# The output projection's first 512 columns computed with tokens as rows and held in PSUM

## The chip, the cores and the metric

The kernel runs on one core of a Trainium2 chip. Its time is the device time of one execution in microseconds (us), the median of three runs. Engines are named as the profile names them: PE is TensorE (PEld its weight loads), DVE is VectorE, ACT is ScalarE, POOL is GpSimd, SP is SyncE, whose queue issues most of the transfers. SBUF is the on-chip memory of 128 partitions; PSUM is the memory of eight banks that PE writes, a bank being 128 partitions by 512 fp32 values.

## What is computed

The reference is one step of a decoder layer: an input projection, a chunked mLSTM branch, a sliding-window attention branch, a gated merge, an output projection, a residual and a layer norm. There are 512 prompt tokens and 8 x 4 = 32 sample tokens, and the model is 2048 wide. The end of it, which the change touches, reads:

```python
y = (sigmoid(g_m) * einsum('btc,cd->btd', br_m, w_proj_m)
     + sigmoid(g_a) * einsum('btc,cd->btd', br_a, w_proj_a))
out = einsum('btc,cd->btd', y, w_out)
return layernorm(DN_ALPHA * x + out, ln_w, ln_b)
```

All inputs are fp32.

## The kernel before

All 544 tokens (T = 512 + 32) go through the projections together. Activations are held with channels on the partitions, `[128 channels, tokens]`, 16 such tiles along k for 2048 channels. An fp32 product is made of three fast products in a rounded fp32 form: an operand is split into a high part, cast by ACT (L208 for weights), and a low part, the difference made by DVE (L209); then high x high, high x low and low x high are added in PSUM.

A plain column tile (`gemm`, L232) takes 128 columns of a weight. It loads them in two halves of 8 k (`load_half`, L197, 128 x 8 x 128 values in pieces of 128 columns, on SP's queue; pool `wr`, three buffers), splits each half (`split`, L202, two buffers each of high and low parts), and issues 8 k x 3 x 2 products a half (`products`, L213): the weights are stationary, and the 544 tokens move as two runs of 272 columns (L218), each into a PSUM bank of its own.

Most column tiles come in pairs of 256 columns (`paired`, L732): each pair is computed by seven half-size products instead of eight, numbered 0 to 6, out of sums of weight blocks and sums of activations. `prepare` (L670) makes the weight sums (DVE L679, and POOL transfers that add, L677) and splits them, up to three products ahead; `half_product` (L691) issues 16 products with the high weight part (L699), then 8 with the low one (L701), all of 272 columns; `gather` (L703) combines the banks on ACT, POOL and DVE. A pair uses three banks.

PSUM is two pools of four banks: `sm` for small results and `bank` for the projections. Background work is written as generators that are started by `spawn` and advanced by `tick` (L134), which the loops over products call. The instructions of each engine are put in order by a scheduler that runs a time model over the program; what is written under `tc.high_priority` (weight preparation, offset `AHEAD`) is drawn ahead. Each engine then executes strictly in that order, and so does SP's queue.

Around the change the program runs like this. The last two merged tiles of y (k = 14, 15) are plain tiles of w_proj_m; meanwhile `back` (L1891) reads the first 14 tiles of y from DRAM and splits them into `yh`, `yl` (hi and lo). Then the output projection begins with four plain tiles of w_out (columns 0 to 511). They only need y itself, and during them `operand_sums` (L1692) reads y again and makes the sums that the pairs need. Each of the four results is copied out of PSUM by ACT (L1919) and stored to DRAM (`d_o`, L1920). Then come four pairs (columns 512 to 1535). In their background `plain_back` (L2059) loads each of the four results again, and `add_residual` (L1950) turns it by PE transposes (L1956 for the four blocks of 128 prompt tokens, L1963 for the 32 samples) and adds it to ALPHA times the rows of x: `z0` (prompt rows, columns 0 to 511) and 32 partitions of `zs` (samples), loaded by `load_rows` (L1940, L1941). The first layer norm statistics follow (L1969). The end of the kernel (columns 1536 to 2047, the norm, the stores) comes after the pairs; three of its column tiles are computed for the prompt with tokens as stationary rows and weights moving, 384 columns at a time (L2049).

Of the kernel before, what the change touches and what calls it, by code (L numbers as in the profile page):

```python
# [21 lines left out]
SEQ = 512  # L22
# [52 lines left out]
def _build(tc, nc, i, o, es):  # L75
# [38 lines left out]
    def ev(n=T):  # L114
        return evp.tile([128, n], F32, tag="ev", name=nm("ev"))
# [27 lines left out]
    def drain():  # L143
        while live:
            tick()
# [86 lines left out]
    def gemm(wv, c0, xh, xl, cols=EVEN, raws=(None, None), every=8, prio=0, before=None, parts=(1, 1),  # L232
             ps=None, behind=None, pins=(None, None), splits=None):
        ps = ps or mm()
        for half in range(2):
            if before:
                before(half)
            if splits:
                products(ps, half, *splits[half], xh, xl, cols, every[half] if isinstance(every, tuple) else every)
                continue  # L240
            raw = raws[half] or load_half(wv, c0, half)
            if prio:
                with tc.high_priority(offset=prio):
# [19 lines left out]
    def whole(tiles):  # L263
        return lambda k, c, w: tiles[k // 4][:, k % 4, c:c + w]
# [1402 lines left out]
    def c5t():  # L1667
        return c5.tile([128, T], F32, tag="c5", name=nm("c5"))
# [218 lines left out]
    tx = pool(esE, "ty", 6)  # L1887
    yh_, yl_ = act_tiles(act, "yh"), act_tiles(act, "yl")
    yh, yl = whole(yh_), whole(yl_)

    def back():  # L1891
        for k in range(14):
            t_ = tx.tile([128, T], F32, tag="ty", name=nm("ty"))
            nc.sync.dma_start(t_[:], d_y[k])
            hilo(t_[:], yh_[k // 4][:, k % 4], yl_[k // 4][:, k % 4])
            if k % 2:
                yield

    spawn(back())
    for ct in range(14, 16):  # L1900
        merge = merged(ct, plain=True)
        sg = merge([p_[:, :HT] for p_ in gemm(wm, ct * 128, bmh, bml, every=4, prio=AHEAD)])
        nc.sync.dma_start(d_y[ct], sg[:])
        hilo(sg[:], yh_[ct // 4][:, ct % 4], yl_[ct // 4][:, ct % 4])
    drain()
    esE.close()

# [4 lines left out]
    tx = pool(esT, "txd", 3)  # L1912
    Y = {}
    spawn(operand_sums(d_y, Y, act3, 3))
    for ct in range(4):
        ps = gemm(wo, ct * 128, yh, yl, every=4, prio=AHEAD)
        ot = ev()
        for p_, o_ in halves(ps, ot):
            A.copy(o_, p_)  # L1919
        nc.sync.dma_start(d_o[ct], ot[:])  # L1920
    drain()
    esT.close()

# [132 lines left out]
                nc.sync.dma_start(d_o[c], o[:])  # L2056
        return end

    def plain_back():  # L2059

        for ct in range(4):
            t_ = c5t()
            with tc.issue_after(state["load"].ins):
                nc.sync.dma_start(t_[:], d_o[ct])
            for _ in range(5):
                yield
            add_residual(ct, t_, 0, 5)
        yield
        stats(0, 4, 0)

# [15 lines left out]
        load_ln()  # L2086

    load_rows(0)
    spawn(plain_back())
# [150 lines left out]
```

## Time and profile before

| | us |
|---|---|
| median of three runs | 2443.71 |
| lowest and highest run | 2440.34, 2447.24 |
| the profiled execution's own time | 2442.73 |
| its span in the profile | 2440.9 |
| four plain tiles of w_out, from the first product | 2236.84 to 2284.6 |
| four pairs of w_out | 2284.8 to 2371.35 |

A line of the profile names the source line, the engine, the operation, and output<-input tiles without buffer numbers, then partitions x elements. In a timeline the first two numbers are start and duration in us. Matmuls are pipelined: a product of 272 columns is shown with 0.29 us, but one starts every 0.125 us, so the distance between starts is what one costs. A fp32 product of full precision shows as two records.

### The profile page before, as it was taken

How to read it: one execution, taken by the hardware profiler on the slowest of the kernel's cores; microseconds unless marked ns; L12 is line 12 of the kernel's file. 1: busy time of each engine (PE TensorE's matmuls, PEld its weight loads, DVE VectorE, ACT ScalarE, POOL GpSimd, SP SyncE). 2: the span in 40 equal slices, each digit the busy share in tenths (PEclk: the TensorE clock that was granted, in tenths of full speed). 3: DMA queues.
4: the chain of work that ended last, by engine and by line, in shares of the span. 5: the costliest groups of instructions: out<-in, count | busy, mean ns of one | idle time of the engine just before them, and what ended most of it. 6: DMA issues, size and time to landing. Idle time of an engine off the chain costs nothing.

```text
span 2440.9 us, 49025 instructions
## 1 busy us (share of the span) xinstructions
PE 2425.6 (99%) x19394; PEld 2372.5 (97%) x19394; DVE 1910.2 (78%) x2879; ACT 1252.0 (51%) x2074; POOL 533.8 (22%) x509
## 2 busy tenths in 40 slices
PE   8999999999999999999999999999999999999998
PEld 8999999999999999999999999999999999999997
DVE  7768888888888888887877888878865676877666
ACT  6456676666666665443433444444654444434432
POOL 3114333333333431211111121120000120111111
PEclk9999999999999999999999999999999999999999
DMA  6876766667767655577687677587864588898776
GB/s 179 197 178 155 164 157 156 153 155 178 167 169 177 164 141 159 153 221 231 192 255 232 174 231 225 174 245 217 264 204 148 186 236 265 233 235 270 199 218 205
DMA packets 569597, 479.88 MB, mean 197 GB/s; under 512 B 48664, under 2 KB 464136, under 8 KB 569112
## 3 DMA queue, kind: packets, MB, share of 16 engines
q1 hardware_dynamic: 550776, 411.22, 56.9%
q0 software_dynamic: 18112, 64.76, 13.5%
q8 instruction: 152, 2.49, 0.4%
q10 hardware_dynamic: 480, 0.79, 0.1%
q14 instruction: 77, 0.63, 0.1%
HBM read 326.35 MB, written 100.77 MB: 175 GB/s over the span
## 4 chain that ended last, share of the span: by engine, by line
PE 97%; DMA 2%; DVE 1%; ACT 0%; issue 0%; SPq 0%; DVEq 0%; POOLq 0%; ACTq 0%
PE bank L699 49%; PE bank L701 24%; PE bank L218 10%; PE sm L1529 2%; PE bank L1335 1%; PE sm L1568 1%; PE sm L814 1%; PE sm L1584 1%; PE sm L865 1%; PE sm L218 1%; PE sm L2049 1%; DMA raw<-raw 1%; PE sm L840 1%; PE sm L1340 1%; DMA raw<-in_w_out 1%; DMA raw<-in_w_proj_a 0%
## 5 line engine op out<-in xcount | busy, mean ns | idle before, releaser
L208 ACT CAST wh<-raw 128x1024 fp32r<-128x1024 f32 x641 | 671.8, 1048 | 822.4 <-PE bank L699 697.1
L209 DVE TENSOR_TENSOR wl<-raw,wh 128x1024 fp32r<-128x1024 f32 x641 | 801.2, 1250 | 198.8 <-ACT wh L208 185.6
L699 PE MATMUL bank<-xk,wh 128*128 128x272 f32 x2336 | 323.4, 289 | 0.0
L679 DVE TENSOR_TENSOR raw<-raw,raw 128x1024 f32<-128x1024 f32 x244 | 310.9, 1275 | 9.7 <-DMA raw<-in_w_proj_a 2.3
L699 PEld LDWEIGHTS bank<-xk,wh 128*128 128x128 f32 x2336 | 303.4, 188 | 1.9 <-issue 1.4
L718 POOL TENSOR_TENSOR ev<-p,ev 128x272 f32<-128x272 f32 x85 | 117.7, 1384 | 453.2 <-ACT ev L717 429.7
L699 PE MATMUL bank<-n2h,wh 128*128 128x272 f32 x656 | 170.0, 291 | 0.0
L699 PE MATMUL bank<-n3h,wh 128*128 128x272 f32 x656 | 169.5, 291 | 0.3 <-ACT wh L208 0.2
L701 PE MATMUL bank<-xk,wl 128*128 128x272 f32 x1168 | 169.8, 287 | 0.0
L699 PE MATMUL bank<-s1h,wh 128*128 128x272 f32 x656 | 169.6, 291 | 0.0
L699 PE MATMUL bank<-n2l,wh 128*128 128x272 f32 x656 | 168.0, 287 | 0.0
L699 PE MATMUL bank<-n3l,wh 128*128 128x272 f32 x656 | 167.6, 288 | 0.0
L699 PE MATMUL bank<-s4h,wh 128*128 128x272 f32 x656 | 167.5, 289 | 0.0
L699 PE MATMUL bank<-s1l,wh 128*128 128x272 f32 x656 | 167.4, 287 | 0.0
L699 PE MATMUL bank<-s4l,wh 128*128 128x272 f32 x656 | 167.0, 287 | 0.0
L701 PEld LDWEIGHTS bank<-xk,wl 128*128 128x128 f32 x1168 | 155.5, 188 | 0.1
L677 POOL DMA_DIRECT2D raw<-raw x96 | 83.2, 866 | 320.3 <-DVE ev L726 209.9
L699 PE MATMUL bank<-a11h,wh 128*128 128x272 f32 x584 | 150.4, 289 | 0.0
L699 PE MATMUL bank<-a11l,wh 128*128 128x272 f32 x584 | 149.4, 288 | 0.0
L699 PEld LDWEIGHTS bank<-n3h,wh 128*128 128x128 f32 x656 | 123.4, 188 | 2.2 <-issue 1.2
L699 PEld LDWEIGHTS bank<-s1h,wh 128*128 128x128 f32 x656 | 123.2, 188 | 1.6 <-issue 1.0
L699 PEld LDWEIGHTS bank<-n2h,wh 128*128 128x128 f32 x656 | 123.4, 188 | 1.2 <-issue 1.2
(552 smaller groups left out, 5800.2 us busy)
## 6 DMA issues: line engine op xcount, KB each, us to landing
raw<-in_w_in SPq DMA_DIRECT2D x296, 512.0 KB
raw<-raw POOLq DMA_DIRECT2D x96, 512.0 KB, 5.0
C<-in_state_mlstm_C SPq DMA_DIRECT2D x32, 1024.0 KB
out<-C SPq DMA_DIRECT2D x64, 512.0 KB
raw<-in_w_proj_a SPq DMA_DIRECT2D x32, 512.0 KB
raw<-in_w_proj_m SPq DMA_DIRECT2D x32, 512.0 KB
raw<-in_w_out SPq DMA_DIRECT2D x32, 512.0 KB
d_v<-ev SPq DMA_DIRECT2D x16, 272.0 KB
```

Source lines behind the costliest of these rows:

```text
L208: state["cast"] = A.copy(wh[:, k:k + n], raw[:, k:k + n])
L209: state["split"] = V.tensor_tensor(out=wl[:, k:k + n], in0=raw[:, k:k + n], in1=r32(wh[:, k:k + n]), op=ALU.subtract)
L218: PE.matmul(ps[f][:, :w], a[:, kk], b(k, c, w), start=(k == 0 and n == 0), stop=(k == 15 and n == 2))
L677: state["summed"] = G.dma_start(out=w[out][:], in_=w[b][:], accum_op=ALU.add)
L679: V.tensor_tensor(out=w[out][:], in0=w[a][:], in1=w[b][:], op=ALU.add)
L699: PE.matmul(ps, wh[:, k], x(p, k), start=(first and k == 0 and p == 0), stop=False, skip_group_check=True)
L701: state["end"] = PE.matmul(ps, wl[:, k], x(0, k), start=False, stop=(k == 7), skip_group_check=True)
L718: G.tensor_tensor(out=c22, in0=p1, in1=c11, op=ALU.subtract)
L814: PE.matmul(pp[:, c0 + w0:c0 + 256], qs[a][:, j * 128:j * 128 + 128], kx[:, k0:k0 + 256 - w0], start=(n == 0), stop=(n == 1))
L840: PE.transpose(pt[:, b * 128:b * 128 + 128], s_[:, b, 128:256], ident)
L865: PE.matmul(po[:, b * 128:b * 128 + n], VA[:, b], p_[:, 2 * b:2 * b + n // 128], start=(b == 0 and m == 0), stop=(b == 3 and m == 1), skip ...
L1529: state["cells"] = PE.matmul(pp[:, 0:258], a[:, b * 128:b * 128 + 128], b_[:, b, f], start=(b == 0 and n == 0), stop=(b == 3 and n == 2))
```

## The change

The four plain tiles of w_out are replaced by one wide stage with tokens as rows:

- The weight is loaded in eight blocks of two k by all 512 columns (`load_wide`, L1921 of the new kernel), the same bytes in pieces of 512 columns instead of 128, into the same three buffers. `split_wide` splits a block as before (cast L1927, difference L1928).
- For each k and each of four blocks of 128 prompt tokens, three products of 512 columns are issued (`row_products`, L1935): 128 tokens of `yh` or `yl` are stationary, the weights move. Each token block has a `sm` bank, all four of that pool, which holds 128 tokens x 512 output columns to the end.
- The 32 samples go apart (`sample_products`, L1939), in full fp32, from the unsplit weights and an fp32 copy of y's sample columns (`y_s32`, filled by 16 small POOL copies, L1897 and L1907). Four products for four successive k stand side by side in four groups of 32 array columns, into the four quarters of a fifth bank. They are issued ahead of steps 0, 2, 4 and 6 of the eight, and need two weight blocks each.
- ACT's copies, the stores to `d_o`, the loads back and the transposes of these four tiles go. `lead_back` adds the four banks directly to ALPHA x `z0` on DVE (L2097), and the four quarters of the fifth one by one to `zs` (L2099, L2101), in the background of the first pair. The statistics follow.

The pairs and the end are written as before.

```diff
+    y_s32 = pool(es, "ys", 1, side="left").tile([128, KT, NS], F32, name="y_s32")
...
             hilo(t_[:], yh_[k // 4][:, k % 4], yl_[k // 4][:, k % 4])
+            G.tensor_copy(y_s32[:, k], t_[:, SEQ:T])
...
-    for ct in range(4):
-        ps = gemm(wo, ct * 128, yh, yl, every=4, prio=AHEAD)
-        ot = ev()
-        for p_, o_ in halves(ps, ot):
-            A.copy(o_, p_)
-        nc.sync.dma_start(d_o[ct], ot[:])
+    def load_wide(c0, j):
+        raw = wr.tile([128, 2, 512], F32, tag="raw", name=nm("raw"))
+        state["load"] = nc.sync.dma_start(raw[:], wo[:, 2 * j:2 * j + 2, c0:c0 + 512])
+        return raw
...
+    def row_products(ps, t, k, w):
+        yk = slice(t * 128, t * 128 + 128)
+        hi, lo = yh_[k // 4][:, k % 4, yk], yl_[k // 4][:, k % 4, yk]
+        for n, (a, p) in enumerate(((hi, 0), (lo, 0), (hi, 1))):
+            state["rows_end"] = PE.matmul(ps[:], a, w[p][:, k % 2], start=(k == 0 and n == 0), stop=(k == KT - 1 and n == 2))
+
+    def sample_products(ps, k0, raws):
+        for c in range(4):
+            PE.matmul(ps[c * 32:c * 32 + 32, :], y_s32[:, k0 + c], raws[c // 2][:, c % 2], start=(k0 == 0),
+                      stop=(k0 == KT - 4), tile_position=(0, c * 32))
+
+    def wide(c0, blocks, ps_s, raws, place, step):
+        for j in range(8):
+            while len(raws) < min(j + 3, 8):
+                raws.append(load_wide(c0, len(raws)))
+            step(j)
+            if j % 2 == 0:
+                sample_products(ps_s, 2 * j, raws[j:j + 2])
+            w = place(j, raws[j])
+            for k in (2 * j, 2 * j + 1):
+                for t, ps in blocks.items():
+                    row_products(ps, t, k, w)
+                tick()
+
+    lead_rows, lead_samples = {t: sm() for t in range(4)}, bank()
+    wide(0, lead_rows, lead_samples, [], lambda j, raw: split_wide(raw, wp, ("wh", "wl")), lambda j: None)
...
-    def plain_back():
-
-        for ct in range(4):
-            t_ = c5t()
-            with tc.issue_after(state["load"].ins):
-                nc.sync.dma_start(t_[:], d_o[ct])
-            for _ in range(5):
-                yield
-            add_residual(ct, t_, 0, 5)
+    def lead_back():
+        for t, ps in lead_rows.items():
+            V.scalar_tensor_tensor(z0[:, t], z0[:, t], ALPHA, ps[:], op0=ALU.mult, op1=ALU.add)
+        yield
+        V.scalar_tensor_tensor(zs[0:32], zs[0:32], ALPHA, lead_samples[0:32], op0=ALU.mult, op1=ALU.add)
+        for c in range(1, 4):
+            V.tensor_tensor(out=zs[0:32], in0=zs[0:32], in1=lead_samples[c * 32:c * 32 + 32], op=ALU.add)
         yield
         stats(0, 4, 0)
```

How the change moves instructions is seen at three places. In these rows the number behind a name tells one tile of that name from another.

The first is PE at the start of the output projection. Before, the first plain tile alternates between its two banks:

```order
L218 MATMUL bank_27454<-yh_27139,wh_27458 128x272
L218 MATMUL bank_27455<-yh_27139,wh_27458 128x272
L218 MATMUL bank_27454<-yl_27143,wh_27458 128x272
L218 MATMUL bank_27455<-yl_27143,wh_27458 128x272
L218 MATMUL bank_27454<-yh_27139,wl_27459 128x272
L218 MATMUL bank_27455<-yh_27139,wl_27459 128x272
```

Now the first sample group stands first, and reads the first two weight blocks, raw_27479 and raw_27481; three products for each of the four token banks follow:

```order
L1939 MATMUL bank_27478<-raw_27479,y_s_27150 32x512 x2
L1939 MATMUL bank_27478<-raw_27481,y_s_27150 32x512 x2
L1935 MATMUL sm_27474<-wh_27489,yh_27139 128x512
L1935 MATMUL sm_27474<-wh_27489,yl_27143 128x512
L1935 MATMUL sm_27474<-wl_27490,yh_27139 128x512
L1935 MATMUL sm_27475<-wh_27489,yh_27139 128x512
```

What moved: the second weight block is read by PE ahead of the first row product, and it is PE as well as the split that frees a block's buffer.

The second place is SP's queue at the end of this stage, before:

```order
L195 DMA raw_27948<-in_w_out 128x8x128
L668 DMA raw_3738_28044<-in_w_out 128x8x128
L668 DMA raw_3739_28046<-in_w_out 128x8x128
L2064 DMA c_3749_28091<-d_o 128x544
L1920 DMA d_o<-ev_27734 128x544
L195 DMA raw_28040<-in_w_out 128x8x128
L195 DMA raw_28042<-in_w_out 128x8x128
L1920 DMA d_o<-ev_27876 128x544
L195 DMA raw_28161<-in_w_out 128x8x128
L1940 DMA z_28034<-in_x_prompt 128x4x512
L1941 DMA zs<-in_x_sample 32x512
```

and now (raw_27715 is the last wide block; raw_27865 and raw_27867 are the first pair's blocks, in the buffers of the sixth and seventh wide block; raw_27996 is the second pair's first one, in the buffer of the eighth):

```order
L1921 DMA raw_27715<-in_w_out 128x2x512
L668 DMA raw_3731_27869<-in_w_out 128x8x128
L668 DMA raw_3732_27871<-in_w_out 128x8x128
L195 DMA raw_27865<-in_w_out 128x8x128
L195 DMA raw_27867<-in_w_out 128x8x128
L195 DMA raw_27996<-in_w_out 128x8x128
L1976 DMA z_27859<-in_x_prompt 128x4x512
L1977 DMA zs<-in_x_sample 32x512
L668 DMA raw_3756_28029<-in_w_out 128x8x128
```

What moved: the stores to and loads from `d_o` are gone; the x rows still stand directly behind the first block of the second pair.

The third place is the first pair on DVE. Before, the low parts of its products 0, 1, 2 and 3 (wl_28049, wl_28055, wl_28061, wl_28094) stand together, and the x rows are not touched until later:

```order
L209 TENSOR_TENSOR wl_28049<-raw_28040,wh_28048 128x1024
L679 TENSOR_TENSOR raw_28040<-raw_3742_28052,raw_3738_28044 128x1024
L209 TENSOR_TENSOR wl_28055<-raw_3742_28052,wh_28054 128x1024
L209 TENSOR_TENSOR wl_28061<-raw_28040,wh_28060 128x1024
L209 TENSOR_TENSOR wl_28094<-raw_3739_28046,wh_28093 128x1024
```

Now the additions to the rows of x stand between the low parts of product 0 (wl_27874) and product 1 (wl_27880):

```order
L209 TENSOR_TENSOR wl_27874<-raw_27865,wh_27873 128x1024
L2099 SCALAR_TENSOR_TENSOR zs<-zs,bank_27478 32x512
L679 TENSOR_TENSOR raw_27865<-raw_3735_27877,raw_3731_27869 128x1024
L2101 TENSOR_TENSOR zs<-zs,bank_27478 32x512
L2097 SCALAR_TENSOR_TENSOR z_27859<-z_27859,sm_27474 128x512
L2097 SCALAR_TENSOR_TENSOR z_27859<-z_27859,sm_27475 128x512
L2101 TENSOR_TENSOR zs<-zs,bank_27478 32x512
L2097 SCALAR_TENSOR_TENSOR z_27859<-z_27859,sm_27476 128x512
L2005 BN_STATS stt<-z_27859 128x6
L2097 SCALAR_TENSOR_TENSOR z_27859<-z_27859,sm_27477 128x512
L2005 BN_STATS stt<-z_27859 128x6
L209 TENSOR_TENSOR wl_27880<-raw_3735_27877,wh_27879 128x1024
```

What moved: a split that waited for nothing but its cast and its weights now stands behind ten operations, of which seven need the x rows and the stage's banks; the next low parts (wl_27886, wl_27921) come behind it.

On PE the same product 1 reads its low part (L701) directly behind its 16 products with the high part before:

```order
L699 MATMUL bank_28098<-s1h_27546,wh_28054 128x272
L699 MATMUL bank_28098<-s1l_27547,wh_28054 128x272
L701 MATMUL bank_28098<-s1h_27546,wl_28055 128x272 x8
L699 MATMUL bank_28131<-n2h_27548,wh_28060 128x272
L699 MATMUL bank_28131<-n2l_27549,wh_28060 128x272
```

Now the 16 high products of product 2 (n2) stand in between:

```order
L699 MATMUL bank_27962<-n2l_27544,wh_27885 128x272
L699 MATMUL bank_27962<-n2h_27543,wh_27885 128x272
L699 MATMUL bank_27962<-n2l_27544,wh_27885 128x272
L701 MATMUL bank_27925<-s1h_27541,wl_27880 128x272 x8
L699 MATMUL bank_27889<-yh_27141,wh_27920 128x272
L699 MATMUL bank_27889<-yl_27145,wh_27920 128x272
```

What moved: PE asks for wl_27880 16 products of 272 columns later than its number would say.

More of the change, by code (lines that the diff above doesn't have):

```diff
@@ L1904, in _build @@
         hilo(sg[:], yh_[ct // 4][:, ct % 4], yl_[ct // 4][:, ct % 4])
+        G.tensor_copy(y_s32[:, ct], sg[:, SEQ:T])
     drain()
@@ L1914, in _build, with split_wide @@
     spawn(operand_sums(d_y, Y, act3, 3))
-    for ct in range(4):
-        ps = gemm(wo, ct * 128, yh, yl, every=4, prio=AHEAD)
-        ot = ev()
-        for p_, o_ in halves(ps, ot):
-            A.copy(o_, p_)
-        nc.sync.dma_start(d_o[ct], ot[:])
+    def load_wide(c0, j):
+        raw = wr.tile([128, 2, 512], F32, tag="raw", name=nm("raw"))
+        state["load"] = nc.sync.dma_start(raw[:], wo[:, 2 * j:2 * j + 2, c0:c0 + 512])
+        return raw
+    def split_wide(raw, p, tags=(None, None)):
+        wh, wl = (p.tile([128, 2, 512], F32R, name=nm(n), **(dict(tag=t_) if t_ else {})) for n, t_ in zip(("wh", "wl"), tags))
+        with tc.high_priority(offset=AHEAD):
+            state["cast"] = A.copy(wh[:], raw[:])
+            state["split"] = V.tensor_tensor(out=wl[:], in0=raw[:], in1=r32(wh[:]), op=ALU.subtract)
+        return wh, wl
+    def row_products(ps, t, k, w):
[21 more added lines that the diff above has]
+    wide(0, lead_rows, lead_samples, [], lambda j, raw: split_wide(raw, wp, ("wh", "wl")), lambda j: None)
     drain()
@@ L2088, in _build @@
     load_rows(0)
-    spawn(plain_back())
+    spawn(lead_back())
     YM = operands((yh_, yl_), Y)
```

## The prediction, made before the change was run

> **What bounds the kernel now.** I read the busy shares first, then the chain of waits, then that chain in order of time around the change.
>
> ```profile
> PE 2425.6 (99%) x19394; PEld 2372.5 (97%) x19394; DVE 1910.2 (78%) x2879; ACT 1252.0 (51%) x2074; POOL 533.8 (22%) x509
> ...
> PE 97%; DMA 2%; DVE 1%; ACT 0%; issue 0%; SPq 0%; DVEq 0%; POOLq 0%; ACTq 0%
> ```
>
> TensorE (PE) is busy 99% of the span and 97% of the chain. The chain in order of time (start, us, what) shows it around the changed stage:
>
> ```profile
> 2212.95 71.84 PE bank L218 x576
> 2284.79 2.02 PE bank L699 x16
> 2286.81 1.00 PE bank L701 x8
> ```
>
> 576 products in 71.84 us are 0.1247 us each, without a gap: the last two column tiles of the gated merge (192), then the four tiles of w_out that the change replaces (384). The paired products follow at 16 in 2.02 us. The windows of the two stages (us, then busy us and instructions of PE, PEld, DVE, ACT, POOL, clock, DMA share, GB/s):
>
> ```profile
> 2236.84:2284.79 47.95, 47.95 (x388) 47.95 (x387) 38.49 (x80) 22.78 (x49) 5.94 (x8) 1.00 0.81 238
> 2284.79:2371.35 86.56, 86.56 (x695) 86.51 (x694) 52.21 (x61) 34.90 (x43) 11.54 (x11) 1.00 0.72 185
> ```
>
> The clock is full in both. So only two things can move the end: PE's own work, and a new wait of PE. Removed transfers and ScalarE (ACT) copies are worth nothing in themselves, because nothing on PE waits for them.
>
> **What PE loses and gains.** The 384 products of 272 columns cost 384 x 0.1247 = 47.9 us. In their place come 192 products of 512 columns (4 blocks of tokens x 16 k x 3). The nearest rows are the products of 384 columns at the end of the kernel, which have the same form (tokens as stationary rows, weights moving):
>
> ```profile
> 2411.65 0.51 PE L2049 MATMUL sm<-w,yh 128*128 128x384 f32 x2
> 2412.00 0.34 PE L2049 MATMUL sm<-w,yl 128*128 128x384 f32 x1
> ...
> 2417.80 0.34 PE L2049 MATMUL sm<-w,yl 128*128 128x384 f32 x1
> 2417.97 0.28 PE L1992 MATMUL sm<-mv,room 128*128 128x2 f32 x2
> ```
>
> Twelve such triples, 36 products, start between 2411.65 and 2417.97: 0.1756 us each. Per column that is 0.457 ns, against 0.458 ns at 272 columns, so the price goes by columns and 512 of them cost 0.234 us: 192 x 0.234 = 44.9 us. The other bound is from durations:
>
> ```profile
> L1568 PE MATMUL sm<-t,t 128*128 128x512 f32 x48 | 11.7, 389 | 0.0
> L1568 PE MATMUL sm<-t,t 128*128 128x384 f32 x48 | 9.1, 337 | 0.0
> ```
>
> 128 more columns lengthen one product by 0.052 us, so the spacing is at least 0.1756 + 0.052 = 0.228 us, 43.7 us in all. I take 44.9, by the rows that were spaced alike.
>
> The Trainium skill ("TensorE: Matmul & The Clock Gate", Back-to-back issue gap) gives N/2.4 + 2.5 ns, 216 ns at 512 columns. By it the stage would be 3.5 us shorter still; but it gives 162.5 ns at 384 columns, where the trace has 175.6, so the trace does not agree.
>
> The samples get 16 products in 4 groups, each of 4 column groups of 32, fp32. The sampled mLSTM state has exactly that form (the line before and the line behind it are shown for the gaps):
>
> ```profile
> 1040.74 0.66 PE L701 MATMUL bank<-xk,wl 128*128 128x272 f32 x4
> 1041.34 1.06 PE L1335 MATMUL bank<-C,qz 128*32 128x512 f32 x8
> 1042.33 0.50 PE L1340 MATMUL sm<-VB,Ab 32*128 32x512 f32 x4
> ```
>
> Four products (8 records) take 0.99 us to the next line's start. The four of L701 should have ended their spacing at 1040.74 + 4 x 0.125 = 1041.24, so entering costs 0.10; I add the same for leaving: 1.2 us a group, 4.8 us. Bounds: 4.0 us without gaps, and 32 records one after another at 0.234 = 7.5 us if the column groups did not overlap.
>
> The Trainium skill ("TensorEngine Tiling (Array Packing)", Key Properties) says that changing the tiling mode drains the TensorE; eight changes speak against the edit. The 0.10 us is what this trace shows of it.
>
> So this stage becomes 44.9 + 4.8 = 49.7 us: 1.8 us longer. Against that stand the transposes that go. They sit in the paired stage, five per tile:
>
> ```profile
> 2301.71 1.17 PE L701 MATMUL bank<-s4h,wl 128*128 128x272 f32 x8
> 2302.72 0.60 PE L1956 MATMUL sm<-cc,c 128*128 128x128 f32 x4
> 2303.15 0.27 PE L1963 MATMUL sm<-cc,c 128*32 128x128 f32 x1
> 2303.18 0.38 PE L699 MATMUL bank<-yh,wh 128*128 128x272 f32 x1
> 2303.39 0.29 PE L699 MATMUL bank<-yl,wh 128*128 128x272 f32 x1
> ```
>
> Without them the second product of the next step would start at 2302.72 + 0.125; it starts at 2303.39: 0.55 us a tile, 2.2 us for four. (Bound from below: the five alone, 0.46 a tile, 1.8 us.)
>
> PE's work is then 1.8 - 2.2 = -0.4 us, between -2.4 (0.228 spacing, 4.0 for samples) and +2.7 (7.5 for samples, 1.8 back).
>
> **The new wait.** Before, tile after tile came back from DRAM late in the paired stage; the first use of the x rows (z, zs) was at 2304.41, 26 us after their issue:
>
> ```profile
> 2277.54 0.37 SPq L195 DMA_DIRECT2D raw<-in_w_out  x1
> 2278.13 2.35 SPq L1940 DMA_DIRECT2D z<-in_x_prompt  x1
> 2280.53 0.72 SPq L1941 DMA_DIRECT2D zs<-in_x_sample  x1
> ...
> 2304.41 0.68 DVE L1957 SCALAR_TENSOR_TENSOR z<-z,sm 128x512 f32<-128x512 f32 x1
> 2305.01 0.27 DVE L1964 SCALAR_TENSOR_TENSOR zs<-zs,sm 32x128 f32<-32x128 f32 x1
> ```
>
> Now VectorE (DVE) adds them in front of the low parts of the second and third product's weights (wl_27880, wl_27886), and executes in order. Let E be the end of the new stage on PE. SP's queue issues the rows behind two weight blocks whose buffers the last sample group and the last split free. Two steps of 24 products follow that group, so it ends at E - 48 x 0.234 = E - 11.2; the first block is issued then. The second waits for the last split, which starts with a cast into the buffer that step 5 frees at E - 12.4:
>
> ```profile
> L208 ACT CAST wh<-raw 128x1024 fp32r<-128x1024 f32 x85 | 89.2, 1050 | 127.7 <-PE bank L699 90.4 <-PE bank L218 11.5 <-DVE c L1854 11.0
> ...
> L209 DVE TENSOR_TENSOR wl<-raw,wh 128x1024 fp32r<-128x1024 f32 x86 | 104.9, 1220 | 43.7 <-ACT wh L208 43.4 <-DMA raw<-in_w_out 0.2
> ```
>
> That is E - 10.1; the rows go directly behind. What the transfers then take follows from their sizes (the z rows are as large as the zr rows) and from the stretches after the issue in the trace before (last two columns DMA share and GB/s):
>
> ```profile
> raw<-in_w_out SPq DMA_DIRECT2D x32, 512.0 KB
> ...
> zr<-in_x_prompt SPq DMA_DIRECT2D x3, 1024.0 KB
> ```
>
> ```profile
> 2278.00:2280.00 2.00, 2.00 (x18) 2.00 (x17) 0.27 (x1) 1.05 (x1) 0.00 (x0) 1.00 1.09 168
> ...
> 2282.00:2284.00 2.00, 2.00 (x18) 2.00 (x17) 0.22 (x1) 0.00 (x0) 0.00 (x0) 1.00 1.13 351
> 2284.00:2286.00 2.00, 2.00 (x18) 2.00 (x17) 0.34 (x1) 1.42 (x3) 0.00 (x0) 1.00 1.03 379
> 2286.00:2288.00 2.00, 2.00 (x18) 2.00 (x17) 0.92 (x2) 1.31 (x3) 0.00 (x0) 1.00 0.56 175
> ```
>
> A weight block (0.52 MB) goes at the first rate, 168 GB/s, 3.1 us; the x rows (1.05 MB) at some 365, 2.9 us. Two blocks and the rows from E - 11.1: E - 2.0; the samples' rows behind them, about E - 0.5. Bounds: with blocks at the high rate too E - 3.7; with the 9.9 us from 2278.13 to the end of that busy stretch E + 1.7. From there DVE has eleven operations up to that low part: 7 of 512 columns, 2 statistics, a sum and the split:
>
> ```profile
> L679 DVE TENSOR_TENSOR raw<-raw,raw 128x1024 f32<-128x1024 f32 x8 | 9.8, 1222 | 0.2
> ...
> L1957 DVE SCALAR_TENSOR_TENSOR z<-z,sm 128x512 f32<-128x512 f32 x4 | 2.7, 680 | 0.0
> L1969 DVE BATCH_NORM_STATS2 stt<-z 128x6 f32<-128x512 f32 x4 | 2.5, 668 | 0.0
> ```
>
> 7 x 0.68 + 2 x 0.67 + 2 x 1.22 = 8.5 us, less some 0.05 of overlap each: 8.0. It is ready at E + 7.5 (E + 4.3 to E + 9.7). PE's new order asks for it after 24 + 16 + 16 products, E + 7.0. The stall is 0.5 us; the fourth product's cast waits for the same split, and so on down the two weight buffers, for which I add 0.5. Together 1.0 us, between 0 and 3.5.
>
> Other waits, at nothing: the splits inside the stage (2.3 us in each step of 5.6); the sample blocks, whose buffers come free 11.2 us before the group that needs them, against 9.9 us for the slowest transfer above; POOL's 16 copies of 32 columns, which stand ahead of its loads when it idles, and are done for k 0 to 3 many us before the first group. If a block came late, each of three groups would pay the excess.
>
> **Sum.** +1.8 - 2.2 + 1.0 = +0.6 us on the profiled execution's 2442.73: 2443.3. That execution lies 1.0 us below the median of 2443.71, so the median goes to 2444.3.
>
> **Rivals.** (a) The x rows come late enough to set the end: each us after E - 0.5 is a us of PE. For the rows to be 8 us later (E + 7.5) they would have to wait behind two more blocks and half of another load; the stall is 9 us, 2452. For: DVE's order puts four products' weights behind them. Against: 26 us of slack before, and a queue with little else in it. It decides from about 7 us of delay. (b) Sample blocks are late by 2 to 3 us at three groups, +7: 2451. For: PE itself must have read a block before its buffer is loaded again. Against: 2 KB rows instead of 512 bytes. (c) The column groups do not overlap or drain at length: +2.7, 2447. (d) The 512-column products are spaced closer than by their columns, at the 0.228 of the durations: -1.2, 2443.1. For: the durations. Against: the even 0.457 and 0.458 ns per column. By the spacing of the Trainium skill's page above ("TensorE: Matmul & The Clock Gate") it would be 2440.8. (e) Something hidden goes away and the gain passes 7 us: I find no gap in PE's rows to regain. That PSUM banks run out is excluded: pairs hold three of four, and the sample bank is freed in the first pair.
>
> **Chances.** Forecast 0.70 (its own range 2441.5 to 2447.5), (a) 0.08, (b) 0.05, (c) 0.07, (d) 0.07, (e) 0.03. A measurement of this kernel (runs from 2440.34 to 2447.24) can tell about 0.3%, 7.3 us, from no change. Slower than 2451.0: (a), (b) in part and a little of (c), 0.14. Faster than 2436.4: (e) and the edge of (d), 0.06. Same: 0.80. The range takes (c) and (d) in and the start of (a): 2439 to 2451.
>
> **What would show it.** The stage of L1935 and L1939 lasts 49.7 us, products 0.234 us apart, groups of L1939 1.2 us. The paired stage is 2.2 us shorter but for one gap of about 1 us before the low products of the second product (L701), released by DVE behind zs and z. A gap ahead of L1939 released by a DMA would speak for (b). The forecast is wrong if the paired stage holds gaps over 4 us, or the stage is under 47 us.

## The result and the profile after

The kernel before takes 2441.68 us (median of 18 runs, 2439.86 to 2447.24), the changed one 2445.51 us (18 runs, 2442.86 to 2452.13). The ratio is 1.0018, with a 95% interval of 1.0011 to 1.0024: 3.8 us longer, between 2.7 and 5.9. That is less than the 0.3% (7.3 us) that the prediction takes as the least that can be told from no change, but the interval leaves out 1. The profiled execution of the changed kernel took 2447.59 us (span 2445.8), 4.9 us more than that of before.

The windows of the changed kernel's trace show the new stage, the four pairs behind it and the tail from column tile 12 to the end (us, busy us and instructions of PE, PEld, DVE, ACT, POOL, clock, DMA share, GB/s):

```profile
2236.24:2285.73 49.49, 49.49 (x225) 36.56 (x225) 36.42 (x79) 20.63 (x41) 6.65 (x10) 1.00 0.76 235
2285.73:2373.14 87.41, 85.16 (x673) 84.57 (x672) 55.07 (x62) 34.53 (x41) 13.02 (x11) 1.00 0.65 159
2373.14:2445.80 72.66, 62.25 (x414) 56.05 (x412) 45.57 (x81) 15.10 (x23) 9.87 (x14) 0.97 0.72 222
```

The same two last stretches in the trace of before:

```profile
2284.63:2371.18 86.55, 86.55 (x694) 86.50 (x693) 52.21 (x61) 34.89 (x43) 11.54 (x11) 1.00 0.72 185
2371.18:2440.90 69.72, 61.85 (x414) 56.04 (x412) 45.38 (x81) 15.19 (x23) 9.86 (x14) 0.97 0.72 226
```

So the 4.9 us are: 0.6 us gained before the stage (in code that is the same), +1.7 in the stage (49.6 us with the 0.09 of entering it, against 47.9), +0.9 in the pairs, +2.9 in the tail. Within the pairs PE was busy without a gap before; now 2.25 us of the stretch are idle.

The new stage is what it was worked out to be. PE's timeline at its first and second group of samples (start, duration):

```profile
2235.90 0.41 PE L218 MATMUL bank<-bh,wl 128*128 128x272 f32 x2
2236.24 1.06 PE L1939 MATMUL bank<-raw,y_s 128*32 128x512 f32 x8
2237.24 0.50 PE L1935 MATMUL sm<-wh,yh 128*128 128x512 f32 x1
2237.57 0.39 PE L1935 MATMUL sm<-wh,yl 128*128 128x512 f32 x1
2237.80 0.40 PE L1935 MATMUL sm<-wl,yh 128*128 128x512 f32 x1
...
2248.30 0.40 PE L1935 MATMUL sm<-wl,yh 128*128 128x512 f32 x1
2248.63 1.07 PE L1939 MATMUL bank<-raw,y_s 128*32 128x512 f32 x8
2249.62 0.50 PE L1935 MATMUL sm<-wh,yh 128*128 128x512 f32 x1
2249.97 0.40 PE L1935 MATMUL sm<-wh,yl 128*128 128x512 f32 x1
```

From 2237.57 to 2248.30 there are 46 steps of 0.2333 us. The second group starts 0.33 us after the last row product, 0.10 later than the next product would; it takes 0.99 us, and the product behind it is followed by a step of 0.35 (2249.62 to 2249.97) instead of 0.23. Together 1.2 us a group. (Forecast: 0.234 and 1.2.)

The waits of PE in the first pair of the changed kernel (engine, line waited for, us in total, times, longest):

```profile
PE bank L699 <- ACT wh L208: 1.4, 1, 1.4
PE bank L701 <- DVE wl L209: 0.9, 1, 0.9
```

The second row is the gap that was foreseen. VectorE's timeline shows it; E, the end of the stage on PE, is 2285.73:

```profile
2285.54 0.68 DVE L2099 SCALAR_TENSOR_TENSOR zs<-zs,bank 32x512 f32<-32x512 f32 x1 [3.09 <-DMA zs<-in_x_sample]
...
2292.52 1.21 DVE L209 TENSOR_TENSOR wl<-raw,wh 128x1024 fp32r<-128x1024 f32 x1
...
2295.58 2.33 DVE L209 TENSOR_TENSOR wl<-raw,wh 128x1024 fp32r<-128x1024 f32 x2
```

The first addition starts at E - 0.2, held by the samples' x rows; the low part of product 1 ends at 2293.73, E + 8.0, and PE takes it at 2293.79, 1.0 us late. The first row is a second gap, which was not foreseen. The chain of waits in order of time leads to it:

```profile
2296.77 1.15 DVE wl L209
2297.92 0.03 POOLq L677
2297.95 0.55 POOL ev L718
2298.50 6.13 DMA raw<-raw
2304.63 0.02 issue
...
2304.73 0.04 ACT wh L208
...
2305.68 1.05 ACT wh L208
2306.73 0.04 issue
2306.77 4.28 PE bank L699 x32
```

POOL's adding transfer (raw<-raw) starts at E + 12.8; before it started at 2292.75, 8.1 us after the end of the old stage. It takes 6.1 us. ScalarE's cast of product 6 waits for it (5.0 us); the cast of the next pair's product 0 stands behind that cast, and PE, which takes that product first, waits 1.55 us.

### The profile page after: what moved, and what is told of

The parts are those of the page before. It is cut to its first block, busy times and chain, and to the rows that moved or that the text cites. A ratio compares the mean times of both kernels' runs of the same rounds, so it can differ in the third digit from the quotient of the medians.

```text
span 2445.8 us, 48660 instructions
## 1 busy us (share of the span) xinstructions
PE 2425.9 (99%) x19214; PEld 2359.3 (96%) x19214; DVE 1911.9 (78%) x2879; ACT 1250.4 (51%) x2066; POOL 538.7 (22%) x525
## 5 line engine op out<-in xcount | busy, mean ns | idle before, releaser
L208 ACT CAST wh<-raw 128x1024 fp32r<-128x1024 f32 x633 | 663.2, 1048 | 817.9 <-PE bank L699 683.5
L679 DVE TENSOR_TENSOR raw<-raw,raw 128x1024 f32<-128x1024 f32 x244 | 309.1, 1268 | 10.2 <-DMA raw<-in_w_in 1.9
L701 PE MATMUL bank<-xk,wl 128*128 128x272 f32 x1168 | 169.8, 287 | 0.0
L701 PEld LDWEIGHTS bank<-xk,wl 128*128 128x128 f32 x1168 | 155.6, 188 | 0.1
L699 PEld LDWEIGHTS bank<-s4h,wh 128*128 128x128 f32 x656 | 123.2, 188 | 1.4 <-issue 1.2
```

What stands on the lines that cost most here:

```text
L208: state["cast"] = A.copy(wh[:, k:k + n], raw[:, k:k + n])
L679: V.tensor_tensor(out=w[out][:], in0=w[a][:], in1=w[b][:], op=ALU.add)
L699: PE.matmul(ps, wh[:, k], x(p, k), start=(first and k == 0 and p == 0), stop=False, skip_group_check=True)
L701: state["end"] = PE.matmul(ps, wl[:, k], x(0, k), start=False, stop=(k == 7), skip_group_check=True)
```

## Experiments

"The stretch" is the time from E to the first product of column tile 12 (the four pairs), "the tail" what follows.

**The changed kernel again.**

> The changed kernel once more, nothing edited, for a second trace and as the mark for the other runs on the same chip. Its first trace is 4.9 us longer than the trace of before: 1.1 us in the new stage, 2.5 us in two gaps of TensorE in the first pair (1.0 and 1.55 us), 1.65 us given back by the transposes left out of three later tiles, and 2.7 us more in the tail between the last pair and the end, where before and after run the same code (69.55 us before, 72.49 us after from the first product of column tile 12 to the end). Theory T1: the loss in the tail is a matter of how the tail's transfers fall in one execution; then the tail of this trace lies anywhere from 69.5 to 73 us, and the two gaps of the first pair are there again within 0.3 us. Theory T2: the change makes the tail longer every time; then it is 72.5 us again, within 0.5. The time over several rounds: 2445.5 us, ratio to before 1.0015 by either.

Measured: 2447.83 us (8 runs), 1.0020 (1.0010 to 1.0030). The tail is 70.1 us this time, so its length differs between executions of one program. The stretch, though, is 90.8 us against 87.4, and the waits of PE in the first pair are not the same two, and far outside the 0.3 expected:

```profile
PE bank L701 <- DVE wl L209: 2.9, 1, 2.9
PE bank L699 <- ACT wh L208: 1.5, 1, 1.5
```

The first row is again the wait for the low part of product 1. The second now stands ahead of product 2, whose cast waited for a sum (L679) that stands behind the first addition on VectorE; at the next pair PE waits for nothing. VectorE's first addition:

```profile
2288.25 0.67 DVE L2099 SCALAR_TENSOR_TENSOR zs<-zs,bank 32x512 f32<-32x512 f32 x1 [7.00 <-DMA zs<-in_x_sample]
```

Here E is 2284.53: the x rows held VectorE until E + 3.7. When they land differs by 4 us between two executions.

**The additions spread out, and put behind two splits.** Work and transfers are as in the change; VectorE's order differs, and with it PE's: the low products of product 1 stand directly behind its high ones again, as in the kernel before. In spread one sample addition stands behind each of four splits, then one row block behind each of the next four:

```diff
     def lead_back():
+        for c in range(4):
+            with tc.issue_after(state["split"].ins):
...
         for t, ps in lead_rows.items():
+            with tc.issue_after(state["split"].ins):
                 V.scalar_tensor_tensor(z0[:, t], z0[:, t], ALPHA, ps[:], op0=ALU.mult, op1=ALU.add)
+                stats(t, t + 1, 0)
+            yield
```

In behind all of them stand behind the split of product 2:

```diff
     def lead_back():
+        with tc.issue_after(state["split"].ins):
             for t, ps in lead_rows.items():
...
```

> The eleven additions and statistics on VectorE are held behind the split of a later product each: one sample addition behind each of four splits, then one row block with its statistics behind each of the next four. Same work, other order. Theory A (order of VectorE's queue): both gaps in the first pair come from the additions standing ahead of the low part of product 1. They go; POOL's subtraction comes at about 6 us after the end of the new stage and its adding transfer directly behind; pairs end 2.5 us earlier against the stage than in after; 2443.0 us, ratio to before 1.0005. Theory B (VectorE's work itself, by what it takes from POOL's and ScalarE's access while it runs densely): the order matters little, gaps of over 1 us in sum stay, 2444.5 to 2445.5 us. The tail: T1, anywhere from 69.5 to 73 us; T2, 72.5 us.

> The eleven additions and statistics stay together, but the first of them waits behind the split of product 2, so that the low parts of products 1 and 2 stand ahead of them; the splits of products 3 to 5 stand in or behind them. Theory A: the first two low parts are on time, so the first gap goes, and with it the delay of POOL's subtraction and of its adding transfer; the split of product 3 moves to some 10 us after the end of the new stage and is asked for at about 11, so no more than 0.5 us of new gap: 2443.0 to 2443.5 us. If a burst of 8 us cannot be hidden in any place, a gap of 1 us or more appears before the low products of product 3 or 4 instead: 2444.5 us. Theory B: POOL's subtraction still takes about 3 us, gaps of over 1 us in sum: 2444.5 to 2445.5.

Measured: spread 2441.53 us (11 runs), 0.9995 (0.9986 to 1.0004); behind 2441.63 us (11 runs), 0.9997 (0.9988 to 1.0006). On the same chip the unedited change took 2447.83. PE waits nowhere in the pairs, and the stretch of spread is

```profile
2284.69:2369.03 84.34, 84.34 (x673) 84.33 (x672) 53.84 (x61) 34.48 (x41) 11.51 (x11) 1.00 0.67 165
```

that is 2.21 us less than the 86.55 of before: the price of the twenty transposes, alone and whole. (behind: 84.77, so the operations together, twelve by the trace, cost 0.4 us in that place.) Theory A holds: the same work in another order loses nothing. It costs more than the 2.5 us that the first trace showed, because that trace was the mildest of the three that were taken with the change's order.

**POOL's subtraction moved to VectorE.** POOL's subtraction took 2.97 us in the changed kernel's trace (1.46 before), directly ahead of the late transfer, and was suspected of holding it.

```diff
-            G.tensor_tensor(out=c22, in0=p1, in1=c11, op=ALU.subtract)
+            (V if w['cA'] == 512 and 'lead' in state else G).tensor_tensor(out=c22, in0=p1, in1=c11, op=ALU.subtract)
```

> The additions stay where the change has them; only the subtraction of the first pair's product 1 goes from POOL to VectorE, so that POOL's adding transfer no longer stands behind it in POOL's queue. Theory A: the first gap (1.0 us, before the low products of product 1) stays, for the low part is as late as in after; the second gap (1.55 us, released by the cast that waited for that transfer) goes, because the transfer's own inputs are ready much earlier: 2444.0 us, ratio to before 1.001. If the second gap comes from something else than POOL's queue (the late low part through the buffers of weights alone, or the DMA queue being slow), it stays at 1 us or more: 2445.5 us.

Measured: 2445.73 us (11 runs), 1.0015 (1.0007 to 1.0024), a stretch of 89.1 us. PE waits once in the first pair, and not at the next pair:

```profile
PE bank L701 <- DVE wl L209: 2.9, 1, 2.9
```

The second gap is gone, but not for the reason that was expected. The x rows landed later in this trace (first addition at E + 1.9), PE lost 3.1 us ahead of the low products of product 1 instead of 1.0, and came to the next pair that much later. The rest of the loss is a slower PE behind that gap. The granted clock (third figure from the end) is

```profile
2297.40:2299.00 1.60, 1.56 (x7) 1.57 (x8) 1.59 (x3) 1.05 (x1) 0.00 (x0) 0.58 0.18 40
2299.00:2301.00 2.00, 2.00 (x11) 2.00 (x10) 2.00 (x3) 0.94 (x2) 0.00 (x0) 0.50 0.77 230
```

and the 16 products from 2297.43 to 2301.07 start 0.23 us apart instead of 0.125, which costs 1.6 us.

With nothing ahead of it on POOL the transfer still starts late, at E + 14.8. What it follows is the split of product 3, whose operand it overwrites (pool_dve first, then behind, where POOL had been free for 3 us):

```profile
2299.23 2.33 DVE L209 TENSOR_TENSOR wl<-raw,wh 128x1024 fp32r<-128x1024 f32 x2
2302.12 0.88 POOL L677 DMA_DIRECT2D raw<-raw  x1 [19.15 <-DMA raw<-in_w_out]
```

```profile
2293.32 1.20 DVE L209 TENSOR_TENSOR wl<-raw,wh 128x1024 fp32r<-128x1024 f32 x1
2295.09 0.89 POOL L677 DMA_DIRECT2D raw<-raw  x1 [2.96 <-issue]
```

The split ends at 2301.56 and 2294.52; the transfer is issued 0.56 and 0.57 us later. In the changed kernel's first trace it is 2297.92 and 2298.50, 0.58. So the expectation's reason was wrong: what makes the transfer late is the split of product 3, and the slow subtraction added nothing.

**The landing of the x rows.** Three kernels change when the rows land. x_ahead issues them before one weight block of the second pair:

```diff
-        nc.sync.dma_start(zs[r], xs_src[:, cs])
+        state["x"] = nc.sync.dma_start(zs[r], xs_src[:, cs])
...
                 if n == 3:
-                    load_a(work[p])
+                    with tc.issue_after(state["x"].ins) if "x" in state else ExitStack():
+                        load_a(work[p])
```

no_x does without them, so that its first 512 columns lack x (the first sample addition is changed in the same way):

```diff
-            V.scalar_tensor_tensor(z0[:, t], z0[:, t], ALPHA, ps[:], op0=ALU.mult, op1=ALU.add)
+            V.tensor_scalar(z0[:, t], ps[:], ALPHA, None, op0=ALU.mult)
...
-    load_rows(0)
     spawn(lead_back())
```

late_x loads them twice:

```diff
     load_rows(0)
+    load_rows(0)
```

> As the changed kernel, but on SP's queue the x rows (z, zs) go ahead of one weight block of the second pair, which stood in front of them; VectorE's order is untouched. Theory L (the landing of the x rows sets the loss): in the three traces with VectorE's order of the change, the first addition started 0.2 us before, 1.9 and 3.7 us after the end E of the new stage, and the stretch from E to the last pair's end took 87.4, 89.1 and 90.8 us, against 84.3 where the additions were spread: a loss of about 3.2 us plus 0.9 us for each us of landing after E. A block less in front should bring the rows some 3 us earlier: landing E - 3 to E + 1, a stretch of 86 to 88 us, 2443.5 us, ratio to before 1.0007. Theory O (only the order on VectorE matters, the landing is a side effect): the stretch stays at 87.5 to 91 us, 2445.5 to 2447.5 us.

> Left out: the x rows of the first 512 columns. The additions keep their place and count on VectorE, but scale the products out of PSUM without adding x, so nothing waits for those two transfers; the four sample operations can then run before E. Theory L: with no landing to wait for, the four row operations and statistics run from about E to E + 4.5, the low part of product 1 is ready at about E + 5.5 and asked for at E + 5.0 to E + 7.0: gaps of 0.5 us at most, a stretch from E to the last pair's end of 84.3 to 85.2 us, 2441.5 to 2442.5 us. Theory O: the burst in front of the low part costs 2 us or more by itself: 86.5 us or more for the stretch, 2444 us.

> The x rows (z, zs) are loaded twice, one load behind the other into the same place, so they land later by one transfer and its wait, some 4 to 6 us; the rest is as in the changed kernel. Theory L: the first addition starts at E + 4 to E + 9, and the loss grows by 0.9 us per us of it: a stretch from E to the last pair's end of 91 to 95 us, 2449 to 2453 us. Theory O: the stretch stays at 87.5 to 91 us, 2445.5 to 2447.5.

Measured: x_ahead 2442.31 us (11 runs), 1.0003 (0.9994 to 1.0012); no_x 2443.44 us (10 runs), 1.0006 (0.9996 to 1.0015); late_x 2447.78 us (10 runs), 1.0025 (1.0016 to 1.0034). VectorE's first addition and the stretch in x_ahead (E is 2283.76):

```profile
2280.97 0.68 DVE L2100 SCALAR_TENSOR_TENSOR zs<-zs,bank 32x512 f32<-32x512 f32 x1 [0.49 <-DMA zs<-in_x_sample]
```

```profile
2283.76:2368.14 84.38, 84.38 (x674) 84.37 (x673) 52.42 (x59) 34.44 (x41) 11.54 (x11) 1.00 0.68 170
```

The stretches of after_again, pool_dve and no_x:

```profile
2284.53:2375.32 90.79, 86.30 (x674) 85.86 (x672) 55.14 (x62) 34.47 (x41) 12.11 (x11) 0.98 0.64 161
```

```profile
2287.33:2376.39 89.06, 86.15 (x674) 85.93 (x673) 55.48 (x63) 34.47 (x41) 10.10 (x10) 0.98 0.65 162
```

```profile
2286.43:2370.76 84.33, 84.33 (x673) 84.33 (x672) 50.16 (x55) 34.49 (x41) 11.49 (x11) 1.00 0.68 166
```

The loss against 84.34 goes with the start of the first addition. The last three columns say where it lies, by the distances between PE's products:

| kernel | first addition | stretch, us | loss, us | waits at products 1 and 2 | wait at the next pair | slower products |
|---|---|---|---|---|---|---|
| no_x | waits for no rows | 84.33 | 0.0 | 0 | 0 | 0 |
| x_ahead | E - 2.8 | 84.38 | 0.0 | 0 | 0 | 0 |
| changed kernel | E - 0.2 | 87.41 | 3.1 | 1.0 | 1.5 | 0.5 |
| pool_dve | E + 1.9 | 89.06 | 4.7 | 3.1 | 0 | 1.6 |
| after_again | E + 3.7 | 90.79 | 6.4 | 4.8 | 0 | 1.6 |

Theory L holds: the loss goes with the landing, though in x_ahead less was left than the 86 to 88 us of stretch that were expected. Theory O falls: x_ahead keeps the order of VectorE and of PE and loses nothing. (no_x says it less cleanly, because there the four sample operations ran ahead of the low part of product 0, and its median lies 0.9 us above the expected range, although its stretch is as expected.)

The parts of the loss change from trace to trace, its sum does not jump. The casts of product 6 and of the next pair's product 0 stand one behind the other on ScalarE, and wait for the adding transfer in x_ahead (the first row) and in pool_dve (the second) as they do in the changed kernel:

```profile
2299.67 2.00 ACT L208 CAST wh<-raw 128x1024 fp32r<-128x1024 f32 x2 [3.17 <-DMA raw<-raw]
```

```profile
2307.68 2.00 ACT L208 CAST wh<-raw 128x1024 fp32r<-128x1024 f32 x2 [3.00 <-DMA raw<-raw]
```

The next pair's weights are then ready at E + 17.9 in x_ahead, where PE takes them at E + 18.1, and at E + 21.0, 22.4 and 24.2 in the changed kernel, pool_dve and after_again. Against E + 18.1 this is 2.9, 4.3 and 6.1 us, nearly the whole loss of each. In the first of the three PE waits for it; in the other two PE was already so late, by its first waits and its slower products, that it came 0.4 and 0.3 us after these weights. By this working, which no run takes apart, the loss begins just behind E - 2.8 and grows by about 1 us per us; no trace has a landing between E - 2.8 and E - 0.2.

late_x is no clean point of the series. Its rows (first addition at E + 5.8) were so late that the scheduler put the split of product 1 ahead of the additions; the burst then fell on products 2 and 3 (gaps of 0.5 and 2.4 us, with a granted clock of 0.57 and 0.53 in the 3.8 us behind them), and the stretch of 89.5 us lies below what was expected.

**Both edits, and a try at the tail.**

> The two edits together: x rows ahead of the second pair's weight block on SP's queue, and the additions behind the split of product 2 on VectorE. Theory L: either edit alone already takes the whole loss away (stretch from E to the last pair's end 84.4 and 84.8 us against 87.4 to 90.8), so the two together give no more: 84.3 to 84.8 us, and a time like theirs, 2441.3 to 2442.3 us, ratio to before 0.9995 to 1.0002. If something of the loss was still left in each, another 0.5 us or more goes: 2440.5 to 2441. Tail: 69.6 to 70.1 us or 70.7 to 73.0, about half and half, as in the eight traces of the changed kernel and its variants.

Measured: 2442.53 us (11 runs), 1.0002 (0.9993 to 1.0011), stretch 84.76, tail 70.5. The two edits together give no more than one. Of the four kernels without the loss (0.9995, 0.9997, 1.0003, 1.0002) none can be told from the kernel before.

In both_moved 64 small products are added behind the first transposes:

```diff
+    for _ in range(64):
+        PE.matmul(warm[:, 0:2], ident, ident[:, 0:2], start=True, stop=True)
```

> As the one with the two edits, and 64 matrix products of two columns more at the very start, where TensorE waits for the first loads; their only purpose is to move the places in TensorE's instruction stream at which a block of instructions is loaded (16 KB by a queue of its own, one every 16 to 18 us at the end of the kernel). In all eight traces with the change such a load falls within 0.3 us of the issue of the first zr rows, 7 us before the tail; in four of them that issue took 1.1 to 1.7 us instead of 0.38, the 2 KB rows behind it moved at 221 to 252 GB/s instead of 370 to 399, and the tail was 70.7 to 73.0 us long instead of 69.6 to 70.1. In the two traces of before the load lies elsewhere and the tail was 69.7 and 69.8. Theory F (the instruction load at that place makes the tail long): with the load about 8 us away the tail is 69.6 to 70.1 us; the median falls by about 1 us below the one without the 64 products, less what these cost at the start (0 to 2 us). Theory N (another cause): a tail over 70.7 us is as likely as before, and the medians differ only by the cost at the start. One trace with a short tail would not settle it, one with a long tail and the load elsewhere would be against F.

Measured: 2468.50 us (4 runs), 1.0106 (1.0093 to 1.0120). The 64 products of two columns cost more than ten times what was allowed for:

```profile
7.17 24.67 PE L309 MATMUL sm<-cc 128*128 128x2 f32 x128
```

```profile
7.17:31.70 24.53, 24.53 (x130) 24.53 (x129) 0.00 (x0) 0.00 (x0) 0.00 (x0) 0.56 0.66 195
```

That is 0.38 us each at a granted clock of 0.56, with everything else of the kernel behind them. And the instruction load did not move: it still fell within 0.3 us of the zr issue. The profile shows a reason: the 64 products are 128 product and 128 weight-load instructions, and the queue that loads instructions moved 152 packets of 16 KB instead of 151. The edit was just one such block long, so the blocks behind it could begin at the same instructions as before. The tail (70.0 us) therefore says nothing about theory F.

**The kernel before, three more traces.**

> The kernel before, unedited, for a second trace. The tail from column tile 12 on took 69.6 to 70.1 us in four of six traces and 72.7 and 73.0 in two (the changed kernel's first trace and that with spread additions), with the same program once so and once so. Theory T1 (how the tail's transfers fall in one execution): 69.7 us or 72.8 us, the short one likelier at 2 to 1; new here would be a long one. Theory T2 (the change lengthens the tail): 69.7 us. A short one tells nothing apart.

> The kernel before, unedited, for a third trace of its tail. In ten traces with the new stage the tail from column tile 12 on took 69.6 to 73.0 us, 70.8 in the mean, over 70.5 in five; in two traces of the kernel before 69.7 and 69.8. Theory T1 (chance, the same in both kernels): over 70.5 us with a chance of one half. Theory T2 (only programs with the new stage have the long tail): 69.6 to 70.1 us.

> The kernel before, unedited, for a fourth trace of its tail, with the same two expectations as for the third: by T1 over 70.5 us with a chance of one half, by T2 69.6 to 70.1 us. Four short ones of four would leave T1 a chance of about 1 in 16.

Measured: tails of 69.76, 69.77 and 70.07 us, beside 69.72 in the first. In the ten traces with the new stage the tail took 69.57 to 72.97 us, 70.8 in the mean. In four of the five long ones (not in the kernel both, 70.5 us) it begins with the first load of zr rows, whose issue took 1.1 to 1.7 us instead of 0.38. SP's queue and the 2 us ahead of the tail in the changed kernel's first trace (72.7 us) and in its second (70.1 us):

```profile
2366.07 1.61 SPq L1976 DMA_DIRECT2D zr<-in_x_prompt  x1
```

```profile
2371.14:2373.14 2.00, 2.00 (x18) 2.00 (x17) 0.77 (x1) 0.80 (x1) 0.00 (x0) 1.00 0.96 244
```

```profile
2368.23 0.38 SPq L1976 DMA_DIRECT2D zr<-in_x_prompt  x1
```

```profile
2373.32:2375.32 2.00, 2.00 (x19) 2.00 (x17) 0.76 (x1) 0.81 (x1) 0.00 (x0) 1.00 1.05 391
```

The same 2 KB rows move at 244 instead of 391 GB/s with the engines as busy. Four short tails of four, against five of ten over 70.5 us, speak for T2, that programs with the new stage have the long tail more often, about 1 us in the mean. That is not shown, and its cause stays open: the coincidence with the instruction load is there in long and short tails alike.

## Why the prediction was right, and where it was not

Forecast 2444.3 us with a range of 2439 to 2451, most of the chance on no change that can be told; measured 2445.51, 0.18% slower. By its steps:

- **PE's work.** Stage 49.7 forecast, 49.6 measured; spacing 0.234 against 0.233; groups 1.2 against 1.2; transposes 2.2 against 2.21 (spread). Rivals (c) and (d) fall: the column groups overlap, and 512 columns cost what columns cost. So does (b): no gap stands ahead of a sample group. The -0.4 us for the sum of PE's work was -0.5. The formula of the Trainium skill ("TensorE: Matmul & The Clock Gate", Back-to-back issue gap) gives 216 ns for 512 columns. It does not hold for these products: the trace has 233.3.
- **The new wait** is the term that was mis-sized: "Together 1.0 us, between 0 and 3.5". The loss was 3.1 us in the first trace, 6.4 in the second. Three parts of it failed.
  First, what follows the late split. The stall for product 1 came out well (the low part at E + 8.0 for a landing at E - 0.2, the gap 1.0 us against 0.5 forecast). But "and so on down the two weight buffers, for which I add 0.5" was 2.1 us in the first trace. The adding transfer, which must wait for the split of product 3 and then takes 6.1 us, was not followed, although it stands in the program's order and in the profile's list of transfers.
  Second, the landing. E - 0.5 was a fair value for the mildest case (E - 0.2), but the other two traces have E + 1.9 and E + 3.7, beyond the upper bound of E + 1.7. The rows were issued at E - 7.3 to E - 8.5, not E - 10.1, since the weight block in front waited for the last split's end. And POOL's first adding transfer (0.5 MB), issued at E - 5.2, ran among them; it was in no line of that budget.
  Third, the prediction prices a wait by its length alone. Behind gaps of about 3 us the granted clock was half for more than 3 us, 1.6 us more in each of the two later traces (most of which PE would otherwise have waited at the next pair).
- **Rival (a)** got 0.08 and a deciding point of 7 us of delay. It was not another case but the same mechanism further along. Its price, a us of PE for each us of landing, was right: the waits at products 1 and 2 are 1.0, 3.1 and 4.8 us for E - 0.2, E + 1.9 and E + 3.7. What was wrong is the deciding point: in the second trace, 4 us behind the forecast landing, PE's waits are 4.4 us by their rows, over the 4 us of gaps by which the prediction would have called itself wrong.
- **The tail** was in no term: +2.9 us in the first trace, about 1 in the mean of ten. A comparison of two single executions takes such differences for effects.

So the median's excess over the forecast, 1.2 us, is not the error of one term: the wait was 2 to 5 us larger in three traces, the kernel before was 2 us shorter over 18 runs (2441.68) than in the three that were shown, and the tail came on top. That the total stayed in the range was partly luck.

## What to carry over

When work is moved onto an engine that feeds the critical one, follow the delayed instruction past its first consumer: here a split that was nearly 5 us late held an in-place adding transfer, and the transfer's 6 us made a second, larger gap some products later. Such a path can set the time without showing as a wait, when the critical engine is already late from something else. Operations that wait for a fresh load belong behind the feeding work in the engine's queue, not in front of it; that order cost at most 0.4 us here, and no landing held PE. A landing time read from one trace is one draw, so leave it a few us, or test the order that doesn't need it.

## What was not expected of the hardware

A long gap of PE costs more than its length. After the gaps of 3.1 us in pool_dve and after_again the granted clock was 0.50 to 0.58 for some 3 to 3.6 us (late_x, after 2.4 us, likewise), and products started 0.23 us apart instead of 0.125; after gaps of 1.0, 1.5 and 1.7 us in the changed kernel's two traces it stayed at 1.00. What length of gap is enough, and what else plays into it, was not measured.

A load can be all but done and still hold its consumer for 3 us. In after_again the x rows were issued at 2277.2 and 2277.9 and released VectorE at 2288.25, but the transfers of that time were all but over by 2285.2 (windows, then the queues of one us: packets, MB, share):

```profile
2283.20:2285.20 2.00, 2.00 (x13) 1.73 (x12) 0.00 (x0) 0.66 (x1) 0.00 (x0) 1.00 1.01 206
2285.20:2287.20 2.00, 2.00 (x18) 2.00 (x18) 0.00 (x0) 0.39 (x1) 0.00 (x0) 1.00 0.08 17
2287.20:2288.20 1.00, 1.00 (x11) 1.00 (x10) 0.00 (x0) 0.00 (x0) 0.00 (x0) 1.00 0.03 8
```

```profile
DMA packets 5, 0.02 MB, mean 16 GB/s; under 512 B 0, under 2 KB 0, under 8 KB 5
...
q0 software_dynamic: 3, 0.01, 6.1%
q1 hardware_dynamic: 2, 0.00, 1.2%
```

From 2286 to 2287 five packets moved, three of POOL's adding transfer (q0) and two of SP's queue (q1), with a share of 7% of 16 engines, about one engine. SP's queue moved its last five packets in the us after that, and none after 2288. The Trainium skill ("DMA: Bandwidth & Descriptors", Why a DMA increments its semaphore by 16 and not by 1) says that a load counts as landed only when each of the engines it was spread over has finished; this trace agrees, with a last engine some 3 us behind. Which engine it was, and whether the adding packets held it up, the profile does not tell.

POOL's subtraction of 128 x 272 took 1.46 us beside ordinary VectorE work and 2.97 us, in after_again 2.06, behind the dense burst. It cost nothing here.
